# A gate's bias as a two-row pass of its product, and weight splits ordered behind a norm

## The chip, the cores and the metric

The kernel runs on one core of one Trainium2 chip. The metric is the time of one execution in microseconds on the device; the time before is the median of three runs. One execution was also profiled, and its trace gives every instruction of each engine: PE (TensorE matmuls; PEld its weight loads), DVE (VectorE), ACT (ScalarE), POOL (GpSimd) and SP (SyncE, which issues nearly all transfers).

## The reference

Two transformer blocks over 256 tokens of width 1024. The first block has two layers, the second one. Each layer of the first block ends in an embedding gate and a norm, and this is where the change lies (`DEPTH = 2`):

```python
for i in range(DEPTH):
    x = layer_norm(ALPHA * x + 0.5 * swiglu(x, ffn_w_in[i, 0], ffn_w_out[i, 0]), ln_g[i, 0], ln_b[i, 0])
    mix = token_mix(x, mix_w_in[i], ...)
    x = layer_norm(ALPHA * x + mix, ln_g[i, 1], ln_b[i, 1])
    x = layer_norm(ALPHA * x + 0.5 * swiglu(x, ffn_w_in[i, 1], ffn_w_out[i, 1]), ln_g[i, 2], ln_b[i, 2])
    ple = jax.nn.sigmoid(x @ ple_w_gate[i] + ple_b_gate[i]) * (p[i] @ ple_w_proj[i])
    x = layer_norm(ALPHA * x + ple, ln_g[i, 3], ln_b[i, 3])
```

The second block normalises `x`, projects it (`x @ w_in_2`), and goes on to attention and a mixture of experts.

## The kernel before

The 256 tokens are two tiles of 128 rows, t = 0 and t = 1; a width of 1024 is two halves of 512, h = 0 and h = 1, or eight slices of 128, k = 0 to 7. Every float32 operand of a large product is split into a high and a low part, and one product is three passes of TensorE (`mm3`, L296: high times high, low times high, high times low). `split` (L302) writes the high part on ACT and the low part on DVE. Weights come in pieces of 1 MB into three buffers `wraw`, are split into `whi` and `wlo`, and the buffer is free for the next transfer once DVE has written the last `wlo`. The first 512 columns of the next stage's first weight, its lead, are split into `ghi` and `glo` ahead of time (`start_next`, `start_rest`).

The embedding gate is `ple` (L986). `ple_project` has left `p @ w_proj` in four tiles `pe` (`ple_pe`). `products(t)` gives `x @ w_gate` in two PSUM banks `ple_o`, 24 passes each. `gated(t)` adds the bias on DVE (L1010, `ple_g`, with the bias rows `ple_b` fetched for all 128 partitions), takes tanh on ACT (L108), and multiplies into `pe` on DVE (L1014), since sigmoid(z) is half of tanh(z/2) + 1. `layer_norm` (L372) is a chain on DVE: add and statistics (L380, L384), centre and gain (L390), seven one-column instructions for the root (L336 to L339), and the last step that writes `x` (L395). `x_to_xT` then transposes the tile on PE (`pt`, L319, two groups of four) and splits it into `xTh` (ACT) and `xTl` (DVE), the operand of the next stage: `gu` of the feed-forward in the first layer, and in the second layer, after another normalisation on ACT and DVE (`ms_sq`, `rms_x`), `pj` of the attention.

What sets the order of the work: each engine has one queue of instructions, and a scheduler fixes the order in each queue when the program is built. `after(ins, o)` adds an order between two instructions to what the data demand. `before_weights` and `hold` use it: the splits of weights that are taken from a piece with `hold` set come behind the instruction that `hold` names. Small tiles (`self.s`) share a ring of 11 buffers.

Of the kernel before, what the change touches and what calls it, by code (L numbers as in the profile page):

```python
# [8 lines left out]
F32 = mybir.dt.float32  # L9
F32R = mybir.dt.float32r  # L10
I32 = mybir.dt.int32
AF = mybir.ActivationFunctionType
ALU = mybir.AluOpType
AX = mybir.AxisListType
PSUM = bass.MemoryType.PSUM
P = 128
# [35 lines left out]
class Net:  # L52
# [98 lines left out]
    def masks(self):  # L151
# [15 lines left out]
        def block(name, src, b, m=None):  # L167
# [20 lines left out]
        g.tensor_tensor(self.m64, self.m64, s16, ALU.subtract)  # L188

        self.early = self.c([P, 2, P], "early")  # L190
        g.memset(self.early, 0.0)
        er = self.early[96:98]
        g.memset(er[:, :, 0:64], 1.0)
        g.affine_select(out=er[:, 0], in_=er[:, 0], compare_op=ALU.is_ge, fill=0.0,
                        base=0, pattern=[[0, P]], channel_multiplier=-1)
        g.affine_select(out=er[:, 1], in_=er[:, 1], compare_op=ALU.is_ge, fill=0.0,
                        base=-1, pattern=[[0, P]], channel_multiplier=1)
        self.csel = []
        for i in range(2):
            m = self.c([P, P], f"csel{i}")  # L200
            g.memset(m, 0.0)
            g.memset(m[i * 64:i * 64 + 64], 1.0)
            self.csel.append(m)
        self.c_eps = self.c([P, 1], "c_eps")
        g.memset(self.c_eps, NORM_EPS)
        self.c_lns = self.c([P, 1], "c_lns")
# [198 lines left out]
    def ffn(self, i, j, lnj):  # L405
# [5 lines left out]
        for c0 in range(0, D_FF, 512):  # L411
# [12 lines left out]

            if c0 == 0:
                pc = self.led, self.piece_k(src(1, 0), kk, cw) + self.piece_k(src(1, kk), kk, cw)
                for t in range(NT):
                    for w in range(2):
                        part(w, t, range(KD), pc[w])
            else:  # L430
                for w in range(2):
                    for k0 in range(0, KD, kk):
                        pc = self.piece_k(src(w, k0), kk, cw)
                        for t in range(NT):
                            part(w, t, range(k0, k0 + kk), pc)
# [550 lines left out]
    def ple(self, i):  # L986
        nc, a = self.nc, self.a
        if "f2" not in self.stages:
            self.ple_in(i)
            self.ple_project()  # L990
        pe, xT = self.pe, self.xT
        w = a["ple_w_gate"][i][:, 512:]
        pcs = self.led, self.piece_k(w[:512], 4, 512) + self.piece_k(w[512:], 4, 512)
        self.start_next()
        bg = self.row(a["ple_b_gate"][i:i + 1], "ple_b")
        gb = self.ln_params(i, 3)
        xTn = self.new_xT() if i < DEPTH - 1 else None
        o = {}

        def products(t):  # L1000
            tt = slice(t * P, t * P + P)
            for h in range(2):
                o[t, h] = self.bank(t, "ple_o")
                for k in range(KD):
                    self.mm3(o[t, h], (xT[0][:, k, tt], xT[1][:, k, tt]), pcs[h][k], k == 0, k == KD - 1)

        def gated(t):
            for h in range(2):
                g = self.s("ple_g")
                ins = nc.vector.tensor_tensor(g, o[t, h], bg[h], ALU.add).ins  # L1010
                if t > 0:
                    self.after(ins, self.ln_end)
                self.tact(g, g, AF.Tanh, scale=0.5)
                nc.vector.scalar_tensor_tensor(pe[t, h], g, 1.0, pe[t, h], ALU.add, ALU.mult)  # L1014

        norm = lambda t: self.layer_norm(t, [pe[t, 0], pe[t, 1]], 2.0, gb, xTn)
        products(0)
        gated(0)
        norm(0)
        products(1)  # L1020
        if xTn is None and self.with_second:
            z = [self.attention_in(t) for t in range(NT)]
            next(z[0])
            gated(1)
            next(z[0], None)
            self.log_behind = self.split_hi
            norm(1)
            self.weave(z[1:])
        else:
            gated(1)  # L1030
            norm(1)
        self.before_weights = ()
        self.start_rest()
        self.xT = xTn
# [944 lines left out]
```

## Time and profile before

| | us |
|---|---|
| median of three runs | 1696.42 |
| lowest and highest of them | 1693.31, 1701.42 |
| the profiled execution, its own time | 1690.66 |
| its span in the trace | 1688.9 |
| mean granted clock of TensorE | 0.987 of full |

The span is what the trace covers; the profiled execution's time is 1.76 us longer. The rows further down come from this trace: a row of a timeline gives the start and the length in us of an instruction (or of several alike in a row, `x8`), and in square brackets the idle time of its engine before it, with what ended it. The output comes before the arrow, the inputs after it.

### The profile page before, as it was taken

How to read it: one execution, taken by the hardware profiler on the slowest of the kernel's cores; microseconds unless marked ns; L12 is line 12 of the kernel's file. 1: busy time of each engine (PE TensorE's matmuls, PEld its weight loads, DVE VectorE, ACT ScalarE, POOL GpSimd, SP SyncE). 2: the span in 40 equal slices, each digit the busy share in tenths (PEclk: the TensorE clock that was granted, in tenths of full speed). 3: DMA queues.
4: the chain of work that ended last, by engine and by line, in shares of the span. 5: the costliest groups of instructions: out<-in, count | busy, mean ns of one | idle time of the engine just before them, and what ended most of it. 6: DMA issues, size and time to landing. Idle time of an engine off the chain costs nothing.

```text
span 1688.9 us, 23445 instructions
## 1 busy us (share of the span) xinstructions
PE 1627.1 (96%) x8655; PEld 1365.6 (81%) x8655; DVE 1315.7 (78%) x2449; ACT 901.2 (53%) x1601; POOL 21.8 (1%) x80
## 2 busy tenths in 40 slices
PE   8999999999999989999999999999898889999998
PEld 6888898888888868888889888888687678787876
DVE  7669888568669786688886676687868869899896
ACT  6543375355543435444563535544466558676774
POOL 1000000000000000000000000000100000000000
PEclk9999999999999999999999999999989989999999
DMA  8667662145558756567541246576443329899995
GB/s 292 202 213 255 197 178 81 51 150 189 185 200 281 245 165 198 176 251 243 174 132 51 100 150 211 198 263 226 153 142 112 128 100 336 314 340 329 364 337 196
DMA packets 175193, 342.39 MB, mean 203 GB/s; under 512 B 12969, under 2 KB 49890, under 8 KB 175074
## 3 DMA queue, kind: packets, MB, share of 16 engines
q1 hardware_dynamic: 175074, 340.84, 59.2%
q8 instruction: 70, 1.15, 0.3%
q14 instruction: 49, 0.40, 0.1%
HBM read 339.76 MB, written 1.05 MB: 202 GB/s over the span
## 4 chain that ended last, share of the span: by engine, by line
PE 87%; DVE 8%; ACT 3%; DMA 1%; issue 1%; SPq 0%; DVEq 0%; ACTq 0%
PE gu L298 10%; PE gu L299 10%; PE gu L300 10%; PE pT L539 7%; PE y L300 5%; PE y L298 5%; PE y L299 5%; PE moe_h L299 3%; PE moe_h L300 3%; PE moe_h L298 3%; DVE wlo L304 2%; PE moe_y L299 2%; PE moe_y L298 2%; PE moe_y L300 2%; PE pt L319 1%; PE pt L449 1%
## 5 line engine op out<-in xcount | busy, mean ns | idle before, releaser
L304 DVE TENSOR_TENSOR wlo<-wraw,whi 128x512 fp32r<-128x512 f32 (+3 forms) x752 | 605.5, 836 | 172.1 <-ACT whi L303 169.4
L303 ACT ACTIVATE whi<-wraw 128x512 fp32r<-128x512 f32 (+3 forms) x752 | 528.0, 746 | 362.5 <-issue 103.9
L298 PE MATMUL gu<-whi,xTh 128*128 128x512 f32 (+1 forms) x736 | 274.8, 373 | 0.0
L299 PE MATMUL gu<-wlo,xTh 128*128 128x512 f32 (+1 forms) x736 | 274.2, 373 | 0.0
L300 PE MATMUL gu<-whi,xTl 128*128 128x512 f32 (+1 forms) x736 | 273.8, 372 | 0.0
L298 PEld LDWEIGHTS gu<-whi,xTh 128*128 128x128 f32 x736 | 138.5, 188 | 23.2
L300 PEld LDWEIGHTS gu<-whi,xTl 128*128 128x128 f32 x736 | 138.5, 188 | 23.1
L299 PEld LDWEIGHTS gu<-wlo,xTh 128*128 128x128 f32 x736 | 138.6, 188 | 22.8
L539 PE MATMUL pT<-xTl,whi 128*128 128x256 f32 x352 | 101.7, 290 | 0.0
L539 PE MATMUL pT<-xTh,whi 128*128 128x256 f32 x352 | 101.6, 289 | 0.0
L539 PE MATMUL pT<-xTh,wlo 128*128 128x256 f32 x352 | 101.5, 289 | 0.0
L298 PE MATMUL y<-whi,hTh 128*128 128x512 f32 x224 | 87.7, 391 | 0.0
L300 PE MATMUL y<-whi,hTl 128*128 128x512 f32 x224 | 87.6, 391 | 0.0
L299 PE MATMUL y<-wlo,hTh 128*128 128x512 f32 x224 | 87.2, 389 | 0.0
L298 PE MATMUL y<-whi,xTh 128*128 128x512 f32 x192 | 75.9, 395 | 1.7 <-ACT xTh L303 1.7
L299 PE MATMUL y<-wlo,xTh 128*128 128x512 f32 x192 | 74.8, 390 | 0.0
L300 PE MATMUL y<-whi,xTl 128*128 128x512 f32 x192 | 74.3, 391 | 0.0
L1093 DVE SCALAR_TENSOR_TENSOR ada<-ada_w,silu_c,ada 128x512 f32<-128x512 f32 x84 | 62.7, 746 | 12.6 <-DMA ada_w<-in_w_ada_dram 12.1
L539 PEld LDWEIGHTS pT<-xTh,whi 128*128 128x128 f32 x352 | 67.4, 191 | 1.2 <-issue 1.2
L539 PEld LDWEIGHTS pT<-xTl,whi 128*128 128x128 f32 x352 | 67.2, 191 | 1.0 <-issue 1.0
L539 PEld LDWEIGHTS pT<-xTh,wlo 128*128 128x128 f32 x352 | 67.4, 191 | 0.5 <-issue 0.5
L1206 DVE SCALAR_TENSOR_TENSOR bias<-rel_m,rel_delta,bias 128x384 f32<-128x384 bf16 x116 | 63.9, 611 | 0.5
(561 smaller groups left out, 3194.7 us busy)
## 6 DMA issues: line engine op xcount, KB each, us to landing
wraw<-in_ffn_w_in_dram SPq DMA_DIRECT2D x88, 1024.0 KB
wraw<-in_ffn_w_out_dram SPq DMA_DIRECT2D x44, 1024.0 KB
wraw<-in_mix_w_in_dram SPq DMA_DIRECT2D x28, 1024.0 KB
ada_w<-in_w_ada_dram SPq DMA_DIRECT2D x96, 256.0 KB
wraw<-in_w_gate_dram SPq DMA_DIRECT2D x20, 1024.0 KB
wraw<-in_w_up_dram SPq DMA_DIRECT2D x19, 1024.0 KB
wraw<-in_w_down_dram SPq DMA_DIRECT2D x19, 1024.0 KB
wraw<-in_mix_w_out_dram SPq DMA_DIRECT2D x8, 1024.0 KB
```

The lines of the kernel that those rows point to most:

```text
L298: mm(out, l[0], r[0], start=start, stop=False)
L299: mm(out, l[0], r[1], start=False, stop=False)
L300: mm(out, l[1], r[0], start=False, stop=stop)
L303: h = self.split_hi = self.nc.scalar.activation(hi, src, AF.Copy).ins
L304: self.mark = self.nc.vector.tensor_tensor(lo, src, hi.bitcast(F32), ALU.subtract).ins
L319: self.nc.tensor.transpose(pt[:, j * P:(j + 1) * P], src[:, (c + j) * P:(c + j + 1) * P], self.ident)
L449: nc.tensor.transpose(pt[:, f * P:f * P + P], h[:, f * P:f * P + P], self.ident)
L539: self.nc.tensor.matmul(o[:, :S], w[:, k], z[:, k], start=k == 0 and n == 0, stop=k == KD - 1 and n == 2)
L1093: z = nc.vector.scalar_tensor_tensor(acc, raw, c, acc, ALU.mult, ALU.add)
L1206: z = nc.vector.scalar_tensor_tensor(b, m, d, b, ALU.mult, ALU.add)
```

## The change

In `ple`, the bias no longer stands on 128 partitions. For each half two rows of it are fetched (`ple_b`, 2 by 512, two copies), ACT copies them rounded to the matmul's type (`ple_bs`), and one DVE instruction (`ple_bp`) makes of the two rows the negative of the rounded bias and of what the rounding left: with the identity's column 1 as a scalar, row 0 is 0 times rounded minus bias, row 1 is rounded minus bias, and the sum of both passes times minus one adds up to the bias within the type's accuracy. A pass of two rows with the constant `minus` (2 by 128, all -1) opens each bank `ple_o`. `gated` then takes tanh from the bank, without the DVE addition; the order behind `ln_end` moves to the multiplication that follows. When a layer follows another layer, `hold` is set to the last instruction of the first tile's norm, and is cleared in `ffn` behind the pieces of its first 512 columns. In `masks`, `csel` becomes two broadcast columns of `blk`, `early` is cleared on two partitions alone, and `minus` is written by DVE.

```diff
--- before.py
+++ after.py
@@ -188,19 +188,16 @@
         g.tensor_tensor(self.m64, self.m64, s16, ALU.subtract)
 
         self.early = self.c([P, 2, P], "early")
-        g.memset(self.early, 0.0)
+        g.memset(self.early[96:98], 0.0)
         er = self.early[96:98]
         g.memset(er[:, :, 0:64], 1.0)
         g.affine_select(out=er[:, 0], in_=er[:, 0], compare_op=ALU.is_ge, fill=0.0,
                         base=0, pattern=[[0, P]], channel_multiplier=-1)
         g.affine_select(out=er[:, 1], in_=er[:, 1], compare_op=ALU.is_ge, fill=0.0,
                         base=-1, pattern=[[0, P]], channel_multiplier=1)
-        self.csel = []
-        for i in range(2):
-            m = self.c([P, P], f"csel{i}")
-            g.memset(m, 0.0)
-            g.memset(m[i * 64:i * 64 + 64], 1.0)
-            self.csel.append(m)
+        self.minus = self.c([2, P], "minus", F32R)
+        nc.vector.tensor_copy(self.minus, self.nones[0:2])
+        self.csel = [self.blk[:, n:n + 1].broadcast_to([P, P]) for n in (0, P - 1)]
         self.c_eps = self.c([P, 1], "c_eps")
         g.memset(self.c_eps, NORM_EPS)
         self.c_lns = self.c([P, 1], "c_lns")
@@ -424,6 +421,7 @@
 
             if c0 == 0:
                 pc = self.led, self.piece_k(src(1, 0), kk, cw) + self.piece_k(src(1, kk), kk, cw)
+                self.hold = None
                 for t in range(NT):
                     for w in range(2):
                         part(w, t, range(KD), pc[w])
@@ -992,7 +990,14 @@
         w = a["ple_w_gate"][i][:, 512:]
         pcs = self.led, self.piece_k(w[:512], 4, 512) + self.piece_k(w[512:], 4, 512)
         self.start_next()
-        bg = self.row(a["ple_b_gate"][i:i + 1], "ple_b")
+        bg = []
+        for h in range(2):
+
+            b, z = self.s("ple_b")[:2], self.s("ple_bs", F32R)
+            nc.sync.dma_start(out=b, in_=a["ple_b_gate"][i:i + 1, h * 512:h * 512 + 512].broadcast_to([2, 512]))
+            nc.scalar.activation(z[:2], b, AF.Copy)
+            bg.append(self.s("ple_bp", F32R)[:2])
+            nc.vector.scalar_tensor_tensor(bg[h], z[:2].bitcast(F32), self.ident[0:2, 1:2], b, ALU.mult, ALU.subtract)
         gb = self.ln_params(i, 3)
         xTn = self.new_xT() if i < DEPTH - 1 else None
         o = {}
@@ -1001,17 +1006,17 @@
             tt = slice(t * P, t * P + P)
             for h in range(2):
                 o[t, h] = self.bank(t, "ple_o")
+                nc.tensor.matmul(o[t, h], self.minus, bg[h], start=True, stop=False)
                 for k in range(KD):
-                    self.mm3(o[t, h], (xT[0][:, k, tt], xT[1][:, k, tt]), pcs[h][k], k == 0, k == KD - 1)
+                    self.mm3(o[t, h], (xT[0][:, k, tt], xT[1][:, k, tt]), pcs[h][k], False, k == KD - 1)
 
         def gated(t):
             for h in range(2):
                 g = self.s("ple_g")
-                ins = nc.vector.tensor_tensor(g, o[t, h], bg[h], ALU.add).ins
+                self.tact(g, o[t, h], AF.Tanh, scale=0.5)
+                ins = nc.vector.scalar_tensor_tensor(pe[t, h], g, 1.0, pe[t, h], ALU.add, ALU.mult).ins
                 if t > 0:
                     self.after(ins, self.ln_end)
-                self.tact(g, g, AF.Tanh, scale=0.5)
-                nc.vector.scalar_tensor_tensor(pe[t, h], g, 1.0, pe[t, h], ALU.add, ALU.mult)
 
         norm = lambda t: self.layer_norm(t, [pe[t, 0], pe[t, 1]], 2.0, gb, xTn)
         products(0)
@@ -1027,6 +1032,7 @@
             norm(1)
             self.weave(z[1:])
         else:
+            self.hold = self.ln_end
             gated(1)
             norm(1)
         self.before_weights = ()
```

The new lines stand three lines higher than the old in the helpers: `split` on ACT is L303 before and L300 after, `mm3` L298 to L300 before and L295 to L297 after, the transposes L319 and L316.

PE's queue, first layer, from the last passes of `ple_p` to the first of `ple_o`; `pt<-ident,x` are the transposes of the second tile from the norm ahead. Before:

```order
L299 MATMUL ple_p<-wlo,pTh 128x512
L300 MATMUL ple_p<-whi,pTl 128x512
L298 MATMUL ple_o<-ghi,xTh 128x512
L299 MATMUL ple_o<-glo,xTh 128x512
L300 MATMUL ple_o<-ghi,xTl 128x512
```

After:

```order
L296 MATMUL ple_p<-wlo,pTh 128x512
L297 MATMUL ple_p<-whi,pTl 128x512
L316 MATMUL pt<-ident,x 128x128 x8
L1009 MATMUL ple_o<-ple_bp,minus 128x512
L295 MATMUL ple_o<-ghi,xTh 128x512
L296 MATMUL ple_o<-glo,xTh 128x512
L297 MATMUL ple_o<-ghi,xTl 128x512
```

The eight transposes stood behind 18 and 19 passes of `ple_o`, and now stand ahead of all of them; so does the bias pass. The second layer has the same rows.

DVE's queue, first layer, from the norm ahead (`x`) to the first use of the bias. Before:

```order
L395 SCALAR_TENSOR_TENSOR x<-ln_r,ln_rstd,ln_b 128x512 x2
L304 TENSOR_TENSOR wlo<-wraw,whi 128x512 x2
L304 TENSOR_TENSOR xTl<-pt,xTh 128x4x128 x2
L304 TENSOR_TENSOR wlo<-wraw,whi 128x512 x4
L304 TENSOR_TENSOR glo<-wraw,ghi 128x512
L1010 TENSOR_TENSOR ple_g<-ple_o,ple_b 128x512
```

After:

```order
L392 SCALAR_TENSOR_TENSOR x<-ln_r,ln_rstd,ln_b 128x512 x2
L301 TENSOR_TENSOR wlo<-wraw,whi 128x512 x3
L301 TENSOR_TENSOR xTl<-pt,xTh 128x4x128 x2
L301 TENSOR_TENSOR wlo<-wraw,whi 128x512 x3
L301 TENSOR_TENSOR glo<-wraw,ghi 128x512
L1000 SCALAR_TENSOR_TENSOR ple_bp<-ple_bs,ident,ple_b 2x512
L301 TENSOR_TENSOR glo<-wraw,ghi 128x512
L1000 SCALAR_TENSOR_TENSOR ple_bp<-ple_bs,ident,ple_b 2x512
```

Behind the norm's `x`, the row of the bias for h = 0 stands after three splits, the two `xTl`, three splits and one of the lead, and that for h = 1 one split later.

DVE's queue, first layer, the end of the first tile's norm inside `ple`. Before:

```order
L338 SCALAR_TENSOR_TENSOR rs_h<-rs_z,ln_ve 128x1
L304 TENSOR_TENSOR wlo<-wraw,whi 128x512
L339 SCALAR_TENSOR_TENSOR ln_rstd<-rs_h,rs_z 128x1
L304 TENSOR_TENSOR wlo<-wraw,whi 128x512
L395 SCALAR_TENSOR_TENSOR x<-ln_r,ln_rstd,ln_b 128x512 x2
L1010 TENSOR_TENSOR ple_g<-ple_o,ple_b 128x512 x2
```

After:

```order
L335 SCALAR_TENSOR_TENSOR rs_h<-rs_z,ln_ve 128x1
L336 SCALAR_TENSOR_TENSOR ln_rstd<-rs_h,rs_z 128x1
L392 SCALAR_TENSOR_TENSOR x<-ln_r,ln_rstd,ln_b 128x512 x2
L1017 SCALAR_TENSOR_TENSOR ple_pe<-ple_g,ple_pe 128x512
L301 TENSOR_TENSOR wlo<-wraw,whi 128x512 x2
```

The splits `wlo` that lay between the steps of this norm (ten from the multiplication of h = 1 to `x`) now come behind it; two of the lead, `glo`, stay in it.

On ACT the row `ple_bs` of h = 0 stands ahead of the two `xTh`, and that of h = 1 behind four splits `whi`; in the second layer one split of the lead comes ahead of the `xTh` as well. On SP the bias of h = 1 and the norm's gain and shift are issued behind the lead and two more pieces of weights (second layer: behind two pieces of the lead and one more).

## Rows read from the trace of the kernel before

**Rows 1.** The page: busy time by engine, and the chain that ended last, by engine.

```profile
PE 1627.1 (96%) x8655; PEld 1365.6 (81%) x8655; DVE 1315.7 (78%) x2449; ACT 901.2 (53%) x1601; POOL 21.8 (1%) x80
...
PE 87%; DVE 8%; ACT 3%; DMA 1%; issue 1%; SPq 0%; DVEq 0%; ACTq 0%
```

**Rows 2.** Timeline of PE, first layer: start, length, engine, line, operation, idle before.

```profile
584.83 0.39 PE L298 MATMUL ple_o<-ghi,xTh 128*128 128x512 f32 x1
...
588.92 0.60 PE L319 MATMUL pt<-ident,x 128*128 128x128 f32 x4
589.27 0.48 PE L298 MATMUL ple_o<-whi,xTh 128*128 128x512 f32 x1
...
607.29 0.39 PE L300 MATMUL ple_o<-whi,xTl 128*128 128x512 f32 x1
610.69 1.29 PE L319 MATMUL pt<-ident,x 128*128 128x128 f32 x8 [3.01 <-DVE x L395]
614.72 0.79 PE L298 MATMUL gu<-ghi,xTh 128*128 128x512 f32 x1 [2.74 <-ACT xTh L303]
```

**Rows 3.** Stretches: busy time of PE, PEld, DVE, ACT, POOL, granted clock, DMA share, GB/s.

```profile
614.70:619.00 4.30, 4.28 (x10) 3.37 (x11) 4.30 (x8) 1.50 (x3) 0.00 (x0) 0.50 0.00 0
1221.60:1226.00 4.40, 4.38 (x13) 4.16 (x14) 4.40 (x9) 4.37 (x9) 4.00 (x7) 0.50 0.00 0
```

**Rows 4.** Timeline of DVE, first layer, where the products run.

```profile
585.30 1.41 DVE L395 SCALAR_TENSOR_TENSOR x<-ln_r,ln_rstd,ln_b 128x512 f32<-128x512 f32 x2
586.62 1.29 DVE L304 TENSOR_TENSOR wlo<-wraw,whi 128x512 fp32r<-128x512 f32 x2
590.18 1.36 DVE L304 TENSOR_TENSOR xTl<-pt,xTh 128x512 fp32r<-128x512 f32 x2 [2.27 <-ACT xTh L303]
591.46 2.48 DVE L304 TENSOR_TENSOR wlo<-wraw,whi 128x512 fp32r<-128x512 f32 x4
```

**Rows 5.** Timeline of ACT, the same stretch.

```profile
585.53 1.67 ACT L303 ACTIVATE whi<-wraw 128x512 fp32r<-128x512 f32 x3
589.55 1.27 ACT L303 ACTIVATE xTh<-pt 128x512 fp32r<-128x512 f32 x2 [2.36 <-PE pt L319]
590.72 1.14 ACT L303 ACTIVATE ghi<-wraw 128x512 fp32r<-128x512 f32 x2
594.32 0.63 ACT L303 ACTIVATE whi<-wraw 128x512 fp32r<-128x512 f32 x1 [2.46 <-DMA wraw<-in_ffn_w_in_dram]
```

**Rows 6.** Timeline of SP's transfers, the same stretch.

```profile
577.40 0.93 SPq L365 DMA_DIRECT2D ple_b<-in_ple_b_gate_dram  x2
...
583.38 0.38 SPq L263 DMA_DIRECT2D wraw<-in_ffn_w_in_dram  x1
...
587.94 0.38 SPq L234 DMA_DIRECT2D wraw<-in_ffn_w_in_dram  x1
```

**Rows 7.** Timeline of DVE, first layer, the first tile's norm.

```profile
598.68 0.68 DVE L1014 SCALAR_TENSOR_TENSOR ple_pe<-ple_g,ple_pe 128x512 f32<-128x512 f32 x1
...
609.20 0.68 DVE L304 TENSOR_TENSOR wlo<-wraw,whi 128x512 fp32r<-128x512 f32 x1
609.80 1.40 DVE L395 SCALAR_TENSOR_TENSOR x<-ln_r,ln_rstd,ln_b 128x512 f32<-128x512 f32 x2
```

**Rows 8.** Timeline of DVE, second layer, the first tile's norm.

```profile
1205.22 0.78 DVE L1014 SCALAR_TENSOR_TENSOR ple_pe<-ple_g,ple_pe 128x512 f32<-128x512 f32 x1
...
1211.31 1.42 DVE L395 SCALAR_TENSOR_TENSOR x<-ln_r,ln_rstd,ln_b 128x512 f32<-128x512 f32 x2
```

**Rows 9.** Timeline of PE, second layer.

```profile
1189.59 0.39 PE L298 MATMUL ple_o<-ghi,xTh 128*128 128x512 f32 x1
...
1216.60 1.87 PE L1240 MATMUL pt<-ident,rms_x 128*128 128x128 f32 x8 [4.17 <-ACT rms_x L1234]
1221.62 0.69 PE L298 MATMUL pj<-ghi,xTh 128*128 128x384 f32 x1 [3.15 <-ACT xTh L303]
```

**Rows 10.** Timeline of the start, DVE.

```profile
6.36 0.69 DVE L304 TENSOR_TENSOR xTl<-pt,xTh 128x512 fp32r<-128x512 f32 x1 [4.07 <-ACT xTh L303]
```

## The prediction

> **What bounds the kernel now.** I read the page first: PE is busy for 96% of the span and holds 87% of the chain that ended last [rows 1]. So a microsecond in which PE does nothing is a microsecond of the kernel, and work taken from DVE or ACT is worth only what PE waited for. The second look is at PE's timeline in the two stages that the diff touches. In the first layer the products of the gate run without a break from 584.83 to 607.29, then PE waits 3.01 us for the first tile's norm, transposes it, and waits 2.74 us for the split [rows 2]. In the second layer it waits 4.17 and 3.15 us at the same place [rows 9]. The third look is at the granted clock behind these waits: 0.50 for 4.3 us and more, so TensorE ran at 1.2 instead of 2.4 GHz [rows 3]. Half of 4.3 us, 2.15 us, is lost there. Last I read DVE, ACT and SP around the start of the products, because the new bias row has to come through all three before PE may begin.
>
> A pass of 512 columns costs 0.229 us at full clock: 95 steps from 584.83 to 607.29 with two groups of four transposes of 0.35 us (588.92 to 589.27) between them [rows 2].
>
> **The change, part by part.**
>
> *The start of the products, first layer.* Before, PE goes straight from `ple_p` into `ple_o` at 584.83, and the second tile's transposes come 18 passes later, when their data are long there [rows 2]. After, the transposes stand first, and then the bias pass, on which every pass behind it in the queue has to wait. When can it run? DVE ends that tile's `x` at 585.30 + 1.41 = 586.71 [rows 4]. A group of transposes starts about 0.2 us after the half of `x` that it reads, and the eight end 0.8 us after `x` (610.69 + 1.29 against 611.20) [rows 2, 7]: 587.5. ACT is done with its splits at 587.20 [rows 5]; then come `ple_bs` and the two `xTh`. The trace has no ACT copy of two partitions; the bounds are nothing and the 0.6 us of a 128-partition one, and I take 0.6, since it has as many columns. `xTh` then ends at 587.8 + 1.27 = 589.1, and the second `xTl` 0.7 us later (591.54 against 590.82) at 589.8 [rows 4, 5]. Behind it DVE has three splits at 0.62 (2.48 for four), one of the lead at 0.6, and the bias row [rows 4]: 589.8 + 1.86 + 0.6 + 0.6 = 592.9. For the bias row the bounds are 0.15 (a one-column step) and 0.7 us; again I take the full one. The lead has landed by then: it was split at 590.72 without a wait [rows 5], and its issue at 583.38 hangs on nothing that moves [rows 6]. So PE starts at 593.0 instead of 584.83: 8.1 us late, less the 0.7 us of transposes that it did meanwhile, 7.4 us net. From 587.5 to 593.0 it stands still, and it stood from 584.8 to 586.2. The gaps of 3.01 + 2.74 and 4.17 + 3.15 us, with transposes between, both left the clock at half [rows 2, 3, 9], so I add 2.15 us; bounds nothing and 2.5.
>
> The Trainium skill, "TensorE: Matmul & The Clock Gate", section "Part 1: The HAM clock gate", says that how many matmuls run slow after an idle time differs from run to run of one kernel. Two gaps of one execution cannot show this; taken at its word it widens the 2.15 us, as the bounds do, and moves no other term.
>
> *Four bias passes* on PE per layer: 4 x 0.229 = 0.9 us, if a pass of two rows takes as long as one of 128 (bounds 0 and 0.9; I take 0.9, since it streams the same columns).
>
> *The second bias row* (h = 1) is issued on SP behind a piece whose buffer is free only when DVE has split the last gate piece, at 591.7. Bounds for its landing: 592.4 at once, or 598.4 if it queues behind that piece (587.94 to 594.32 is 6.4 us for one piece) [rows 5, 6]. Then ACT and DVE, 599.7 at the latest; PE wants it after 25 passes, at 593.0 + 5.7 + 2.15 = 600.9. Hidden, with 1 us to spare at half clock, and 1 us short at full clock. Gain and shift (`ln_g`, `ln_b`) are wanted ten microseconds later: nothing.
>
> *The first tile's norm, first layer.* This is what the order is meant for. Before, from the start of the last multiplication to the end of `x` took 609.80 + 1.40 - 598.68 = 12.5 us, with ten `wlo` in it [rows 7]. In the second layer, with none, the same steps took 1212.73 - 1205.22 = 7.5 us [rows 8]. After: 7.5 + two `glo` at 0.6 = 8.7 us, and the DVE addition is gone, so that it starts 0.8 us (tanh and its start) behind the products. These end at 593.0 + 50 x 0.229 + 2.15 = 606.6; `x` ends at 616.1, its first half at 615.4. PE reaches the transposes, 36 passes into the second tile, at 614.8: it waits 0.8 us, does both groups (0.7) and the other 14 passes, and begins `gu` at 619.5, with `xTh` and `xTl` hidden behind these passes. Before, `gu` began at 614.72 and lost 2.15 us at half clock, as good as 616.9. So here +2.6 us: the wait behind the products is nearly gone, 5.75 + 2.15 us, and the wait ahead of them, the clock and the passes cost more.
>
> *The second tile, first layer.* Its norm takes the splits that were moved. From the tanh at 620 the steps with eight splits and one `ffn_h` between them make about 12.2 us, so `x` ends near 632.7; PE comes to its transposes 52 passes after 619.5, at 631.4. I take 1.0 us of waiting; bounds 0 and 3. First layer in all: +3.6 us.
>
> *Second layer.* All rows lie 604.76 us later (1189.59 against 584.83) [rows 2, 9]. A split of the lead of 0.5 us now comes ahead of the `xTh`: the products start 8.6 us late, less 0.7. Two bias passes make 0.46 and the clock 2.15. The first tile's products end at 1198.2 + 11.45 + 2.15 = 1211.8, against 1201.3 before. Then 0.8 + 7.5 + three `glo` at 0.48 = 9.8 us instead of 11.4 (1201.3 to 1212.73) [rows 8]. `x` ends at 1221.5, 8.8 us late, and `pj` follows 8.9 us behind `x` as before [rows 8, 9]: +8.8 us. The old gap does not absorb it, because PE waits there for this very chain; only its work on the second tile fits into it.
>
> *The rest at nothing.* `minus` is one DVE copy at the start, where DVE idles 4.07 us for the first tile [rows 10]; POOL, 1% busy [rows 1], loses four fills and has nobody waiting. The broadcast `csel` are four small passes in all.
>
> **Sum:** 3.6 + 8.8 = 12.4 us. On the profiled execution 1690.66 + 12.4 = 1703.1; it lies 5.8 us under the median of the runs, so for the median 1696.4 + 12.4 = 1708.8, say 1709 us.
>
> **Rivals.**
> - *Cheap stall.* The clock does not fall at the two starts (-4.3), and the second tile waits for nothing (-1.0): +7.1 us, 1704. For it: the stall is cut by 1.3 us of transposes. Against it: both gaps of [rows 2, 9] are cut so as well, and both cost the clock [rows 3].
> - *Faster: PE does not stand at the bias pass.* The norm pays and the stall doesn't come, because PE runs other passes past the waiting one, or because the row is there in time. The point is 585.1: only if the first `ple_bp` were done by then would PE lose nothing. Then `gu` would start at 584.83 + 100 x 0.229 + 1.4 = 609.1, or 7.8 us earlier than 616.9, and the second layer gains 1.6 less 0.46: -8.9 us, 1687.5. Against it: DVE's idle 2.27 us ahead of `xTl`, with four splits behind it whose `whi` ACT had finished at 587.20 [rows 4, 5], shows that a queue is not left out of order there; for PE no row shows it. The Trainium skill, "TensorE: Matmul & The Clock Gate", section "Part 2: What happens when you issue a matmul", says that PE pulls weight loads ahead but leaves the matmuls in program order. By that the sum above holds; if matmuls could pass too, it would be this rival. No run here shows which.
> - *Weights late.* The held splits free two buffers late, so that by the times above the next pieces for `gu` are issued only near 610 and 620, and PE waits in the feed-forward too: one landing time of 6.4 us more, 1715. Against it: PE reaches the first of them 36 passes behind 619.5, at 627.7, 18 us after 610.
>
> **How the numbers follow.** The forecast has 0.65, the cheap stall 0.18, weights late 0.11, faster 0.06. The low end is the cheap stall less the 3.1 us from the median to the lowest run, 1700; the high end is weights late and 2 us of the open bounds, 1717; only the faster case and some of the ends lie outside. A measurement can tell about 0.5%, 8.5 us, from no change: that is 1704.9. Slower by more: 0.6 of the forecast's 0.65 and all of weights late, 0.71. Within: the cheap stall and 0.05, 0.23. Faster: 0.06.
>
> **What would show it.** Right: the first `ple_o<-ple_bp` starts near 593 in the first layer and 1198 in the second, with some 5 us of idle PE ahead of it that DVE's `ple_bp` ended, and the clock at half for 4 us behind it; in the first layer the gap behind the products is under 2 us; `pj` starts near 1230. Wrong: the bias pass within 2 us of `ple_p`; full clock behind a gap of 5 us; new waits of PE on `wlo` or `whi` in `gu`; a two-partition step on ACT or DVE of 0.2 us, which would bring the start to 592.

## The result, and the profile after

| kernel | median of its executions | lowest to highest | the profiled execution | its span |
|---|---|---|---|---|
| before | 1698.6 us (6) | 1693.3 to 1701.4 | 1690.7 us | 1688.9 us |
| after | 1713.1 us (6) | 1709.5 to 1721.8 | 1715.1 us | 1713.4 us |

After is slower: the ratio is 1.0094, with a 95% interval of 1.0065 to 1.0122. That is 16 us, 11 to 21 (the medians of the table differ by 14.5), where the prediction had 12.4 us and 1709 us.

The page of after, with the rows that answer to [rows 1]: PE is busy for 18 us more, and its share of the chain fell from 87 to 84%, because DVE and DMA hold more of it.

```profile
PE 1645.2 (96%) x8663; PEld 1374.8 (80%) x8663; DVE 1315.1 (77%) x2446; ACT 902.6 (53%) x1605; POOL 22.7 (1%) x76
...
PE 84%; DVE 9%; ACT 3%; DMA 3%; issue 1%; SPq 0%; DVEq 0%; ACTq 0%
```

PE's timeline of after in the first layer (start, length, engine, line, operation, idle time before and what ended it), the place of [rows 2]:

```profile
585.01 1.03 PE L316 MATMUL pt<-ident,x 128*128 128x128 f32 x8
592.78 0.79 PE L1009 MATMUL ple_o<-ple_bp,minus 2*128 2x512 f32 x1 [6.74 <-DVE ple_bp L1000]
...
601.99 0.50 PE L1009 MATMUL ple_o<-ple_bp,minus 2*128 2x512 f32 x1
...
608.09 0.50 PE L1009 MATMUL ple_o<-ple_bp,minus 2*128 2x512 f32 x1
...
617.01 0.60 PE L316 MATMUL pt<-ident,x 128*128 128x128 f32 x4
...
621.10 0.39 PE L295 MATMUL gu<-ghi,xTh 128*128 128x512 f32 x1
...
633.68 1.29 PE L316 MATMUL pt<-ident,x 128*128 128x128 f32 x8 [0.63 <-DVE x L392]
```

The eight transposes stand ahead of the products, and then PE waits 6.74 us for the bias row. The gaps of 3.01 and 2.74 us of [rows 2] are gone: the first tile's transposes, at 617.01, find their data there and lie inside the products. The first bank, bias pass and 24 products, takes 592.78 to 601.99, or 9.21 us; the second takes 6.10 us (601.99 to 608.09). So the clock behind the stall costs 3.1 us.

The second layer, the place of [rows 9]:

```profile
1200.28 1.08 PE L316 MATMUL pt<-ident,x 128*128 128x128 f32 x8
1208.34 0.79 PE L1009 MATMUL ple_o<-ple_bp,minus 2*128 2x512 f32 x1 [6.97 <-DVE ple_bp L1000]
...
1216.99 0.50 PE L1009 MATMUL ple_o<-ple_bp,minus 2*128 2x512 f32 x1
...
1235.99 1.27 PE L1246 MATMUL pt<-ident,rms_x 128*128 128x128 f32 x8 [0.65 <-ACT rms_x L1240]
1240.59 0.45 PE L295 MATMUL pj<-ghi,xTh 128*128 128x384 f32 x1 [3.33 <-ACT xTh L300]
```

The wait for the bias row is 6.97 us, and the first bank takes 8.65 us, 2.55 more than 6.10. The old wait of 4.17 us shrank to 0.65, but the one behind it, 3.15 in [rows 9], is still 3.33 us. Stretches of after behind the two stalls (length, busy time of PE, PEld, DVE, ACT and POOL, granted clock, DMA share, GB/s) show the clock at half, as [rows 3] do behind the old gaps:

```profile
592.70:599.70 7.00, 6.92 (x16) 5.16 (x17) 1.37 (x3) 2.00 (x4) 0.00 (x0) 0.51 0.85 298
1208.30:1214.30 6.00, 5.96 (x14) 4.42 (x15) 2.60 (x5) 0.63 (x1) 0.00 (x0) 0.53 1.00 286
```

DVE's timeline of after, where [rows 4] stand, shows why the row is late. ACT had copied it by 587.9, but on DVE its last step stands behind `xTl`, three `wlo` and one `glo`, and it is done at 592.73:

```profile
588.38 1.29 DVE L301 TENSOR_TENSOR xTl<-pt,xTh 128x512 fp32r<-128x512 f32 x2 [1.31 <-ACT xTh L300]
589.59 1.89 DVE L301 TENSOR_TENSOR wlo<-wraw,whi 128x512 fp32r<-128x512 f32 x3
591.39 0.69 DVE L301 TENSOR_TENSOR glo<-wraw,ghi 128x512 fp32r<-128x512 f32 x1
592.00 0.73 DVE L1000 SCALAR_TENSOR_TENSOR ple_bp<-ple_bs,ident,ple_b 2x512 fp32r<-2x512 f32 x1
...
597.61 0.74 DVE L1000 SCALAR_TENSOR_TENSOR ple_bp<-ple_bs,ident,ple_b 2x512 fp32r<-2x512 f32 x1 [4.28 <-ACT ple_bs L998]
```

**What the two stages cost.** To compare traces I take, for each layer, PE's time from the end of `ple_p` to a mark behind the stage: the second group of `ffn_h` transposes (662.52 before, 667.83 after) and the first `lat` transposes (1255.03 before, 1273.62 after). In after the first layer takes 5.1 us longer and the second 7.9: 13.0 us. (Where PE waits behind `ple_p`, its end is a modelled one; that moves a figure by 0.3 us at most.) The pair of profiled executions differs by 24.5 us. The other 11.5 lie where the diff changes nothing, nearly all in stretches at a lower clock.

How much of a time is clock can be read from the executions themselves. Over the 72 executions of before in the experiments below, a line of time against the mean granted clock gives 1697.2 us at 0.981 and 1.28 us less for each 0.001 more; the executions scatter about it by 1.4 us. One more execution of before, of 2032 us at a mean clock of 0.746, is left out of the line and of all ratios. At the same clock after is 13.6 us slower, with 1.0 to either side. This is a comparison at one clock and not a cause, since a stall lowers the mean clock too; but it agrees with the 13.0 us of the two stages.

### The profile page after: what moved, and what is told of

It is laid out like the page before. It is cut to its first block, busy times and chain, and to the rows that moved or that the text cites. A ratio compares the mean times of both kernels' runs of the same rounds, so it can differ in the third digit from the quotient of the medians.

```text
span 1713.4 us, 23451 instructions
## 1 busy us (share of the span) xinstructions
PE 1645.2 (96%) x8663; PEld 1374.8 (80%) x8663; DVE 1315.1 (77%) x2446; ACT 902.6 (53%) x1605; POOL 22.7 (1%) x76
## 4 chain that ended last, share of the span: by engine, by line
PE 84%; DVE 9%; ACT 3%; DMA 3%; issue 1%; SPq 0%; DVEq 0%; ACTq 0%
PE gu L295 9%; PE gu L297 9%; PE gu L296 9%; PE pT L537 7%; PE y L297 4%; PE y L296 4%; PE y L295 4%; PE moe_h L296 3%; PE moe_h L297 3%; PE moe_h L295 3%; DVE wlo L301 2%; PE moe_y L295 2%; PE moe_y L296 2%; PE moe_y L297 2%; PE pj L295 1%; DMA ada_w<-in_w_ada_dram 1%
## 5 line engine op out<-in xcount | busy, mean ns | idle before, releaser
L300 ACT ACTIVATE whi<-wraw 128x512 fp32r<-128x512 f32 (+3 forms) x752 | 527.6, 746 | 355.4 <-issue 104.2
L295 PE MATMUL gu<-whi,xTh 128*128 128x512 f32 (+1 forms) x736 | 274.7, 373 | 0.0
L297 PE MATMUL gu<-whi,xTl 128*128 128x512 f32 (+1 forms) x736 | 273.5, 372 | 0.0
L297 PEld LDWEIGHTS gu<-whi,xTl 128*128 128x128 f32 x736 | 138.7, 189 | 23.1
L295 PEld LDWEIGHTS gu<-whi,xTh 128*128 128x128 f32 x736 | 138.7, 188 | 23.1
L295 PE MATMUL y<-whi,hTh 128*128 128x512 f32 x224 | 87.7, 391 | 0.0
L297 PE MATMUL y<-whi,hTl 128*128 128x512 f32 x224 | 87.7, 391 | 0.0
L295 PE MATMUL y<-whi,xTh 128*128 128x512 f32 x192 | 75.8, 395 | 1.7 <-ACT xTh L300 1.7
L297 PE MATMUL y<-whi,xTl 128*128 128x512 f32 x192 | 74.3, 390 | 0.0
L1099 DVE SCALAR_TENSOR_TENSOR ada<-ada_w,silu_c,ada 128x512 f32<-128x512 f32 x84 | 62.8, 747 | 12.3 <-DMA ada_w<-in_w_ada_dram 11.7
```

What stands on the lines that cost most here:

```text
L295: mm(out, l[0], r[0], start=start, stop=False)
L297: mm(out, l[1], r[0], start=False, stop=stop)
L300: h = self.split_hi = self.nc.scalar.activation(hi, src, AF.Copy).ins
L1099: z = nc.vector.scalar_tensor_tensor(acc, raw, c, acc, ALU.mult, ALU.add)
```

## The experiments

The theory was that the bias row comes late, and that PE's wait for it with the half clock behind it makes the loss. Rival A was that the held splits make it (weights late), rival B that the two-row passes do. The table has all runs. "Timed" is the ratio times 1696 us; "same clock" is read off the line above, with two standard errors; "stages" is the time of the two stages against the first trace of before. The last row is the same program as before, so 2.6 us is how far the stages of two traces of one program can lie apart.

| kernel | timed against before, us | same clock, us | first layer | second layer | stages |
|---|---|---|---|---|---|
| after | +16 (11 to 21) | +13.6 ± 1.0 | +5.1 | +7.9 | +13.0 |
| hold_alone | +0.8 (-2.7 to 4.4) | +0.5 ± 0.9 | -4.3 | -1.5 | -5.7 |
| bias_alone | +21 (16 to 27) | +13.5 ± 0.7 | +4.6 | +7.8 | +12.3 |
| bias_prio | +4.8 (1.2 to 8.3) | +5.1 ± 0.6 | -2.9 | +1.5 | -1.4 |
| bias_last | +10 (6.4 to 13.4) | +6.2 ± 0.8 | +2.9 | +2.0 | +4.9 |
| bias_early | +3.7 (0.2 to 7.3) | +6.3 ± 0.7 | -5.0 | -1.2 | -6.3 |
| early2 | -1.7 (-5.4 to 2.2) | +0.7 ± 0.7 | -5.1 | -1.4 | -6.4 |
| early2_128 | -1.9 (-4.9 to 1.4) | -0.9 ± 0.8 | -5.5 | -1.9 | -7.4 |
| early2_128_nohold | -1.7 (-5.1 to 1.5) | -0.1 ± 1.0 | -3.2 | -1.9 | -5.2 |
| bias_twice | +14 (10 to 18) | +14.3 ± 0.8 | +4.8 | +8.2 | +13.0 |
| rows128 | +16 (12 to 20) | +12.2 ± 0.8 | +3.9 | +7.1 | +10.9 |
| warm | +14 (9 to 19) | +16.5 ± 0.8 | +2.1 | +8.4 | +10.5 |
| before_again | one execution, 1697.9 us | | -2.5 | -0.1 | -2.6 |

**The two parts of the change apart.** hold_alone is before with the two lines on `hold`; bias_alone is after without them.

```diff
 # hold_alone, against before; bias_alone leaves these two out of after
+                self.hold = None          # in ffn, behind the first pieces
+            self.hold = self.ln_end       # in ple, ahead of gated(1)
```

> The kernel before with the order of the splits alone (the lead's splits of the next weights held behind the first tile's x, first layer); the gate's bias stays an addition on DVE. Theory (the late bias row is what costs, the held splits pay): 3 to 7 us below before, most likely 5; in the first layer the waits of 3.01 and 2.74 us behind the products nearly vanish and the products still start right behind ple_p. Rival A (the held splits free their buffers late and the feed-forward waits for weights): 3 us or more above before. Rival B (the price is the four two-row passes themselves): 0 to 5 us below, so this run can't tell B from the theory.

> The kernel after without the order of the splits: only the bias as a two-row pass. Theory: about 20 us above before, as the 15 of the change and some 5 that the held splits gave; rival A: about 8 us above, since the held splits would be half of the loss; rival B: 15 to 20, as the theory. First layer: the bias pass opens the products late, and the gap behind them is back.

bias_alone is as slow as after or slower, and in its trace PE waits 6.68 us for `ple_bp` in the first layer and 6.96 in the second. So the bias is the whole loss, and rival A falls: at the same clock after and bias_alone differ by 0.1 us. One part of the expectation failed: the gap behind the first layer's products is not back. PE's timeline of bias_alone:

```profile
623.92 0.50 PE L295 MATMUL gu<-ghi,xTh 128*128 128x512 f32 x1 [0.74 <-ACT xTh L300]
```

Seven `wlo` still lie in this norm on DVE, and from the last multiplication to the end of `x` it takes 11.7 us (610.75 to 622.41), against 8.3 in after (608.87 to 617.19). Yet PE finds the first half of `x` there when its products are done (622.07), and 0.74 us is all that is left of 5.75. So in after the gap would be nearly gone without the order of the splits too.

hold_alone is a miss. Its trace does what was expected, transposes at 608.67 inside the products and no gap behind them, but PE then waits in `gu` for low halves that DVE splits later than before:

```profile
608.67 0.60 PE L319 MATMUL pt<-ident,x 128*128 128x128 f32 x4
...
616.98 0.50 PE L299 MATMUL gu<-wlo,xTh 128*128 128x512 f32 x1 [1.01 <-DVE wlo L304]
618.18 0.50 PE L299 MATMUL gu<-wlo,xTh 128*128 128x512 f32 x1 [0.23 <-DVE wlo L304]
620.90 0.50 PE L299 MATMUL gu<-wlo,xTh 128*128 128x512 f32 x1 [1.08 <-DVE wlo L304]
```

These 2.3 us are "weights late" in small. They are already in the -4.3 of the first layer, so they don't explain why the times show no gain; before_again does, in part (below).

**The row ahead of its neighbours.**

```diff
 # bias_prio, against after
-        for h in range(2):
+        with self.later(-1000):
+            for h in range(2):
             ... the four instructions of the row, unchanged
```

> The kernel after, but the instructions that make the two bias rows rank ahead of their neighbours, so that the first of them stands on DVE ahead of the norm's x instead of behind xTl, three wlo and one glo; the bias pass still opens the bank. Theory: PE's idle time ahead of the first bias pass falls to under 2 us, and the time lies between 4 us below and 4 above before. Rival B: 8 us or more above before, as the four passes are still there.

PE's wait fell to 1.97 us in each layer, and the time to 4.8 us above before, just outside the 4 below to 4 above that were expected: 11 of the 16 us came back with the passes as they were. What is left has moved to DVE, where the row now waits for ACT at the head of the queue and holds up the norm behind it: DVE idles for 4.30 us, and the norm's `x` begins 3.7 us behind the end of `ple_p` (588.27 to 591.97), in after 1.2 us ahead of it:

```profile
589.45 0.74 DVE L1001 SCALAR_TENSOR_TENSOR ple_bp<-ple_bs,ident,ple_b 2x512 fp32r<-2x512 f32 x1 [4.30 <-ACT ple_bs L999]
```

**The pass at the end of its bank.**

```diff
 # bias_last, against after
-                nc.tensor.matmul(o[t, h], self.minus, bg[h], start=True, stop=False)
                 for k in range(KD):
-                    self.mm3(..., pcs[h][k], False, k == KD - 1)
+                    self.mm3(..., pcs[h][k], k == 0, False)
+                nc.tensor.matmul(o[t, h], self.minus, bg[h], start=False, stop=True)
```

> The kernel after, but the two-row pass closes each bank where it opened it; nothing else changes. The row then has 24 passes more to come, so PE need not wait for it. Theory: the stall of some 7 us at both starts and the half clock behind it are gone, the four passes stay: 6 us below to 1 above before, most likely 3 below. Rival B (the passes themselves): 8 us or more above before. Rival A: 5 us or more above before.

A miss: +10 us, as rival B had it, but the trace shows another cause. The stall at the start is gone (the products follow `ple_p` at 585.16), but the first tile's banks close later. The second bias pass starts at 602.46 (its row leaves DVE at 600.97), and on ACT the tanh of both halves now stands behind splits that wait for buffers which PE's later passes free:

```profile
605.93 1.15 ACT L300 ACTIVATE whi<-wraw 128x512 fp32r<-128x512 f32 x2 [0.85 <-PE ple_o L297]
606.99 1.07 ACT L108 ACTIVATE ple_g<-ple_o 128x512 f32<-128x512 f32 x2
```

PE then waits 5.04 us for `x`. This run moved the late row instead of hiding it, and so it tells the theory from rival B only in part.

**The row early.** The same instructions, written at the start of `ple_in` (bias_early) or at its end (early2), with buffers of another pool.

```diff
 # bias_early: this block ahead of the load of p_in; early2: behind its transposes
+        self.bg = []
+        for h in range(2):
+            b, z = self.g("ple_b")[:2], self.g("ple_bs", F32R)
+            ... load, Copy and scalar_tensor_tensor as in after, into self.g("ple_bp", F32R)[:2]
 # in ple
-        bg = []
-        ... the same block
+        bg = self.bg
```

> The kernel after, but both bias rows of a layer are loaded, split and kept in other buffers some 30 us earlier, beside the products of the feed-forward ahead; the two-row pass still opens each bank. Theory (the late row is what costs): PE goes from ple_p into the bias pass without a wait, the transposes come back inside the products, and of the change the passes stay, 6 of them at 0.64 us on the path, less one DVE addition of 0.7 us a layer and less what the held splits give: 2 us below to 5 us above before, most likely 2 above. Rival B (the passes themselves cost, or something else of the new form): 10 us or more above before, as with the pass at the end.

> As the kernel with the early bias rows, but each row is loaded behind p_in instead of ahead of it: in that run's trace PE waited 2.94 us for p_in, and lost 1 us of clock behind it, in each layer. Theory: these 4 us a layer go, so 8 us under that run, which is 4 below before (8 below to 1 above). If the early rows were no cure and that run's 4 above came from the passes, it stays 2 to 6 above before.

bias_early came in as expected, +3.7 us (6.3 at the same clock). PE goes from `ple_p` into the bias pass without a wait, and the transposes are back inside the products. Its own price is that `p_in` was loaded behind the row; in PE's timeline:

```profile
555.76 1.09 PE L316 MATMUL pt<-ident,p_in 128*128 128x128 f32 x4 [2.94 <-DMA p_in<-in_p_dram]
...
590.02 0.50 PE L1009 MATMUL ple_o<-ple_bp,minus 2*128 2x512 f32 x1
```

early2 has that wait no more and is 1.7 us under before, which the measurement can't tell from no change. PE's timeline of early2, first and second layer:

```profile
589.35 0.50 PE L1009 MATMUL ple_o<-ple_bp,minus 2*128 2x512 f32 x1
...
612.06 1.03 PE L316 MATMUL pt<-ident,x 128*128 128x128 f32 x8
...
1188.90 0.50 PE L1009 MATMUL ple_o<-ple_bp,minus 2*128 2x512 f32 x1
```

With the passes as in after and the row early, the whole loss is gone: 13 us at the same clock. early2 also takes its buffers from another pool, but bias_prio, with the buffers of after, has 8.5 of the 13.6 us back at the same clock. That settles the cause: it is the lateness of the row.

**What a two-row pass costs.** PE's timeline of after around the second bias pass, and the weight loads beside it (PEld):

```profile
601.67 0.39 PE L297 MATMUL ple_o<-whi,xTl 128*128 128x512 f32 x1
601.99 0.50 PE L1009 MATMUL ple_o<-ple_bp,minus 2*128 2x512 f32 x1
602.42 0.50 PE L295 MATMUL ple_o<-whi,xTh 128*128 128x512 f32 x1
602.76 0.39 PE L296 MATMUL ple_o<-wlo,xTh 128*128 128x512 f32 x1
```

```profile
601.45 0.19 PEld L297 LDWEIGHTS ple_o<-whi,xTl 128*128 128x128 f32 x1
601.99 0.18 PEld L1009 LDWEIGHTS ple_o<-ple_bp,minus 2*128 2x128 f32 x1 [0.35 <-issue]
602.42 0.19 PEld L295 LDWEIGHTS ple_o<-whi,xTh 128*128 128x128 f32 x1 [0.24 <-issue]
```

Three intervals take 1.09 us; at 0.229 a pass they would take 0.69. So a bias pass adds 0.64 us, not 0.23. The loads show where: those of the 128-row passes run ahead in step, one in 0.23 us, but the load of the two-row pass stands 0.35 us later than the last one ended, and the one behind it 0.24 us. Two kernels tell the rows from the passes:

```diff
 # bias_twice, against after (minus holds -0.5)
+                nc.tensor.matmul(o[t, h], self.minus, bg[h], start=False, stop=False)   # behind the first
 # rows128, against after: b, z and bp with all 128 partitions, minus 128x128 with -1/64
-            nc.vector.scalar_tensor_tensor(bg[h], z[:2].bitcast(F32), self.ident[0:2, 1:2], b, ...)
+            nc.vector.scalar_tensor_tensor(bg[h], z.bitcast(F32), self.blk[:, P - 1:P], b, ...)
```

> The kernel after with every bias pass done twice, each with the weight -0.5: eight more two-row passes, six of them on the path. At 0.64 us each (as the first trace of after has it for the one pass): 3.8 us above after, so about 20 above before; at 0.23 us each, as a 128-row pass: 1.4 above after. In the trace: four intervals around a later bias pass take 1.7 us by the first and 1.3 by the second.

> The kernel after with a bias pass of 128 rows instead of two: 64 rows of the high part and 64 of the low part, each with the weight -1/64, on DVE and ACT the same instructions with 128 partitions. If a pass of two rows is dear because of its two rows, the three intervals around it fall from 1.09 to 0.69 us and the time lies 2.5 us under after; if it is dear for another reason (the change of the weights from one kind to another), both stay as in after. If the small instructions on DVE and ACT cost by their columns, the first bias pass opens no later than in after.

In bias_twice two such passes stand together, and the second adds only 0.25 us (26 passes in 6.35 us against 25 in 6.10). In PE's timeline:

```profile
602.89 0.49 PE L1009 MATMUL ple_o<-ple_bp,minus 2*128 2x512 f32 x1
603.23 0.39 PE L1010 MATMUL ple_o<-ple_bp,minus 2*128 2x512 f32 x1
603.55 0.50 PE L295 MATMUL ple_o<-whi,xTh 128*128 128x512 f32 x1
```

In rows128 the passes have no such gap; PE's timeline, then its weight loads:

```profile
600.67 0.40 PE L297 MATMUL ple_o<-whi,xTl 128*128 128x512 f32 x1
600.91 0.40 PE L1009 MATMUL ple_o<-ple_bp,minus 128*128 128x512 f32 x1
601.14 0.39 PE L295 MATMUL ple_o<-whi,xTh 128*128 128x512 f32 x1
601.37 0.39 PE L296 MATMUL ple_o<-wlo,xTh 128*128 128x512 f32 x1
```

```profile
600.45 0.19 PEld L297 LDWEIGHTS ple_o<-whi,xTl 128*128 128x128 f32 x1
600.68 0.19 PEld L1009 LDWEIGHTS ple_o<-ple_bp,minus 128*128 128x128 f32 x1
600.91 0.19 PEld L295 LDWEIGHTS ple_o<-whi,xTh 128*128 128x128 f32 x1
```

Three intervals take 0.70 us. So what is dear is the change between 128 rows and two, 0.41 us for the two changes around a pass, and not a pass. In the times neither kernel differs from after: 2 us are under what these intervals resolve. rows128's stages are 2.1 us shorter than after's, near the 2.5 expected; bias_twice's are the same, where 1.5 (six passes of 0.25) more were to come. The row of 128 partitions opens the products hardly later (592.47, which is 8.0 us behind `ple_p`, against 7.8 in after): `ple_bs` takes 0.62 us with 128 partitions and 0.61 with two, `ple_bp` 0.74 and 0.73, so these two instructions cost the same at either height.

> The last kernel with the bias pass of 128 rows. Theory: the 0.41 us that each pass of two rows took beyond a pass of 128 go, six on the path: 2.5 us under the last kernel, 6 below before (10 below to 1 below). Rival: the rows' loads are now of 128 partitions, 256 KB each, and come in the way of the weights: at or above the last kernel.

> The last kernel without the order of the splits. If the held splits give the 4 us that the trace of that order alone showed in its stage, 4 above the last kernel, so 2 below before. If they give nothing that the times show, as that kernel's times had it, the same as the last kernel.

early2_128 is early2 with that form, and early2_128_nohold is the same without the order of the splits. All three lie 1.7 to 1.9 us under before, each within the interval of no change. The stages say 0.9 us for the 128 rows and 2.2 for the held splits; the times show neither.

**The clock behind the stall.**

```diff
 # warm, against after: ahead of products(0), behind the last transpose; the bank is never read
+        warm = self.mm_bank("warm")
+        for _ in range(20):
+            nc.tensor.matmul(warm, self.pT[0][:, 0, 0:P], self.pT[0]..., start=True, stop=True)
```

> The kernel after with 20 more passes of 128 rows on data that are there (their sums are never read), put between the transposes and the first bias pass, so that PE works through most of its wait for the bias row. Theory (half clock behind the stall costs 3.4 us in the first layer and 2.5 in the second): the passes behind the bias pass run at full clock, and the time lies 5 to 6 us under after, 10 above before. Rival C (the clock loses as much elsewhere, or the extra passes themselves hold up the bias pass): within 2 us of after.

In the first layer the extra passes leave 0.87 us of idle time, and the first bank takes 6.03 us (592.73 to 598.76), so the products run at full clock. In the second layer 2.52 us of idle time stay, and the first bank takes 9.09 us:

```profile
592.73 0.47 PE L1009 MATMUL ple_o<-ple_bp,minus 2*128 2x512 f32 x1 [0.87 <-DVE ple_bp L1000]
...
1206.44 0.76 PE L1009 MATMUL ple_o<-ple_bp,minus 2*128 2x512 f32 x1 [2.52 <-DVE ple_bp L1000]
```

The first layer's stage is 3.0 us shorter than in after, as the 3.1 us of half clock had it; the second is not. The times show 2 us of gain in an interval of 10, so they decide nothing between the theory and rival C.

**Before once more.**

> The kernel before once more, for another trace of it. Nothing changes: 1689 to 1703 us. The theory that the clock's drops near 808 to 820 and 1339 to 1344 us, seen in after and in half of the experiments and not in the first trace of before, come by chance with the execution expects one of them here in two cases of three; if they hang on the change, neither is here.

The same program, 7.2 us slower. Outside the two stages it is 9.8 us longer than the first trace of before, nearly as much as the 11.5 us of after, so those 11.5 need not come from the change. Of the two drops named it has none near 1340, and one near 820: 1.7 us are lost at half clock between 821 and 825. The first trace has none there. after, bias_alone, bias_twice, rows128 and warm lost 3.4 us there, but so did early2_128, in which PE never waits for the row. So the drops near 820 need no late row, and one of them comes without the change; whether the change makes them more frequent stays open. Two other drops, which the first trace had not, lie near 204 us (3 us) and under `ple_p`; the one under `ple_p` after has too. The stretch of before_again, where the first trace of before has 1.00:

```profile
583.00:592.00 9.00, 9.00 (x29) 7.23 (x30) 8.61 (x25) 2.39 (x5) 0.00 (x0) 0.65 1.03 351
```

And its first layer is 2.5 us shorter, though nothing in it changed:

```profile
617.59 1.94 PE L319 MATMUL pt<-ident,x 128*128 128x128 f32 x8 [3.02 <-DVE x L395]
619.36 0.80 PE L298 MATMUL gu<-ghi,xTh 128*128 128x512 f32 x1
```

The gap of 2.74 us of [rows 2] isn't there. In the first trace ACT's four `whi` began at 612.00 and stood ahead of `xTh`, which came at 614.10. In this one ACT did these splits while PE still waited for `x`, and `xTh` followed the transposes. ACT's timeline of before, then of before_again:

```profile
607.03 2.19 ACT L303 ACTIVATE whi<-wraw 128x512 fp32r<-128x512 f32 x4 [3.54 <-DMA wraw<-in_ffn_w_in_dram]
612.00 2.19 ACT L303 ACTIVATE whi<-wraw 128x512 fp32r<-128x512 f32 x4 [2.78 <-PE pt L319]
```

```profile
612.16 2.19 ACT L303 ACTIVATE whi<-wraw 128x512 fp32r<-128x512 f32 x4 [1.78 <-DMA wraw<-in_ffn_w_in_dram]
615.83 2.19 ACT L303 ACTIVATE whi<-wraw 128x512 fp32r<-128x512 f32 x4 [1.48 <-DMA wraw<-in_ffn_w_in_dram]
```

SP issued the two pieces equally far behind the start of the products in both traces, 15.2 and 18.8 us (599.99 and 603.65 before, 606.88 and 610.55 here). The splits of the first piece began 7.0 us after its issue in the first trace and 5.3 here, those of the second 8.4 and 5.3. So the first piece landed earlier against PE's work here; for the second piece the first trace names PE's transposes, and not the transfer, as what ended ACT's wait, so that its landing was the cause there too is not shown.

## Why the prediction was right, and where it was not

**The mechanism held.** The first `ple_o<-ple_bp` starts at 592.78, foreseen near 593; the idle time ahead of it is ended by DVE's `ple_bp`; the clock is at half behind it; the gap behind the first layer's products is gone, though bias_alone has next to none of it either, without the order to which the prediction put it; `pj` starts at 1240.59, 10.6 us later than "near 1230", but after is 10.7 us behind already at the end of that layer's `ple_p` (1200.28 against 1189.59), by the first layer and the clock between. The second layer's first bias pass, at 1208.34 instead of 1198, is late for the same reason. Counted from the end of `ple_p`, the first layer cost 5.1 us (3.6 foreseen) and the second 7.9 (8.8): 13.0 against 12.4. The sum hides errors on both sides, so that it is this close is partly luck; against before_again's stages the two layers would be 15.6:

- *The start of the products* was right: 592.78 - 585.01 = 7.8 us late against 8.1, and 8.06 against 8.6 in the second layer. `ple_bs` took 0.61 and `ple_bp` 0.73 us, the upper ends of the bounds, as chosen. The idle time is one piece instead of two, since after's `x` (583.86 to 585.27) was there when PE came to the transposes.
- *The bias pass* was mis-sized: 0.64 us, outside the bounds of 0 and 0.229 for each. That is 1.6 us more in the first layer and 0.8 in the second. The step of the sum that failed is "a pass of two rows takes as long as one of 128": the row it rested on has only passes between others of the same height. The Trainium skill, "TensorEngine Tiling (Array Packing)", section "Key Properties", says that changing the tiling mode drains the TensorE. The late weight loads in after, and their absence with 128 rows, agree with that; that the array drains there, or that a pass of two rows is such a change of mode, no row shows. The 0.41 us should have been a term of the sum.
- *The clock* was mis-sized: 3.1 and 2.55 us, against 2.15 with a bound of 2.5. The Trainium skill, "TensorE: Matmul & The Clock Gate", section "Part 1: The HAM clock gate", says that the number of slow matmuls at a kernel's start differs from run to run of one kernel. No two runs here show that behind one and the same wait: after's first layer lost 3.1 us behind 6.74 us of waiting and bias_alone's 2.6 (8.73 against 6.10) behind 6.68, but these are two kernels.
- *What the norm gave back* was sized too low in the second layer: from the end of the first tile's products to `rms_x`' transposes it took 12.9 us instead of 15.3, 2.4 us gained against 1.6.
- *The second tile* waited 0.63 us (1.0 foreseen), and the second bias row was hidden: ready at 598.35, wanted at 601.99.

**The rivals.** The cheap stall fell: the clock dropped at both starts. PE did stand at the bias pass in every kernel that gave it a late row. Weights late did not show in after, where PE waits for no `wlo` or `whi` in `gu`; it shows where there is no stall and PE is earlier, in hold_alone, with 2.3 us instead of 6.4.

**What the order of the splits is worth** the prediction read from one execution, as a gap of 5.75 us and its clock. Of that 2.74 us hang on where ACT's splits fall, as before_again shows. Against that trace hold_alone's stages gain 3.2 us. The times show no gain: at the same clock it is 0.5 us slower, with 0.9 to either side, and after against bias_alone and early2_128 against early2_128_nohold differ by under 1 us. So the order does what it says and is worth little, also because the gap that it was to close is down to 0.74 us in bias_alone without it; where hold_alone's 3 us of stage go was not settled.

## What to carry to other kernels

When an operand made by three engines opens an accumulation, it sets the start of all passes behind it in PE's queue: make it a stage earlier, behind the loads that PE needs before it, or leave the bias as the addition behind the products that it was. To close the accumulation with it was no cure here (bias_last, +10 us). Moving it ahead of its neighbours only moves the wait: to DVE in bias_prio, to `p_in` in bias_early. And take the price of a gap from more than one execution: the same program had 2.74 us of it in one and none in another.

## What the runs showed of the hardware that was not expected

A matmul of two rows between matmuls of 128 rows costs 0.64 us, one beside another of two rows 0.25, one of 128 rows 0.23: the two changes cost 0.41 us, and the weight loads behind the changes start 0.35 and 0.24 us late. The same sum with the rows spread over all 128 partitions costs nothing extra. Of the scatter of some 15 us between executions of the kernel before, most goes with the mean granted clock, 1.28 us for each 0.001, and 1.4 us of scatter is left about that line.
